# New order tables for TensorE, ScalarE, VectorE and GpSimd in a one-core encoder layer

## The chip, the cores and the metric

The kernel runs on one core of a Trainium2 chip. The metric is the device time of one execution in microseconds; of several executions the median is given. Below, TensorE (PE) does the matrix products, VectorE (DVE), ScalarE (ACT) and GpSimd (POOL) the elementwise work, and SyncE (SP) issues nearly all transfers between the core's memory and DRAM.

## The reference

One layer of an encoder for 1024 new frames ("prompt") and 64 further frames ("sample") that attend to a cache of 512, width 1024, all in float32. Cut to what matters:

```
z = x @ w_in                       # 1024 -> six fox heads (q, k, v, forget gate), u and v of a gated
                                   # unit, six stick-breaking heads (q, k, v)
o_f = softmax(q k / 8 + c_q - c_k) v          # c = cumsum of log forget gates, causal
o_s = sigmoid(z) * prod(1 - sigmoid(later z)) v   # stick-breaking weights, strictly causal
o_g = gelu(u) * (tril(w_s) layer_norm(gelu(v)) + b_s)   # within chunks of 128 positions
o   = rms_norm_per_head([o_f, o_g, o_s]) * g_mix
x   = layer_norm(ALPHA * x + o @ w_out)
h   = square(relu(x @ w_up))                  # 1024 -> 4096
y   = layer_norm(ALPHA * x + h @ w_down)      # 4096 -> 1024
```

Outputs are y for both groups of frames, the new keys and values, the log forget gates and the gated unit's v.

## The kernel before

Every float32 factor is split in a high and a low part, and a product is three passes on TensorE (`PASSES`, L23): high by high, high by low, low by high. ScalarE writes the high part (L1507, L1790), VectorE or GpSimd subtracts it to get the low part (`lo_sub`, L327).

The program is one function, `_build`, whose stages follow one another in time with some overlap:

- 0 to about 520 us: input projection (L613), attention of both kinds (scores L813, transposes L861, products with the values L871 to L874) and the gated unit;
- 520 to 620 us: output projection (L485), residual and first layer norm;
- 620 to 980 us: the up projection (L1569). The 4096 columns go in 16 groups of 256. The frames are in two parts, x = 0 with 288 rows of a product's output and x = 1 with 256. A group's 2 by 2 blocks are multiplied in seven products instead of eight, `PROD` (L1547), into four PSUM accumulators zA to zD per group and part;
- 980 to 1311 us: the down projection (L2034) in a similar scheme, with sums in `acc`;
- to the end: second layer norm of the last tiles and their stores.

The names in the rows below say group and part: zD4_0 is accumulator D of group 4, part 0. In the up stage, `Chain.product` issues the twelve matmuls of a product and then evacuates. The first two products into zA are copied by ScalarE to sn (L1580), the third to a plane of hh for part 0, else to sn (L1580 too). zB is added to sn by VectorE (L1585), zC is subtracted (L1587). zD holds two products in turn: after the first, VectorE adds it to the third copy (L1583), and then the second is accumulated onto it and evacuated by L1589. So the second product into a zD can't start before L1583 has read it. Then relu and square (L1601), four sums and differences of planes (L1610 to L1613), and stores of the planes to DRAM by SyncE (L1614, L1615, L1618), from where the down stage loads them. The buffers hh and sn are used again by later groups, so an evacuation can wait for a store to land. Weights are loaded to wr (L1759), summed by VectorE (L1516 to L1520), and split to wa (ScalarE, GpSimd) and ws (ScalarE L1790, VectorE L327).

In the tail, VectorE adds the last product to acc with a row sum (L2044), takes the negative mean (L2108), ScalarE sums the squares (L2113), GpSimd computes the scale (L2103, L2104) and the shift (L2124), and the row is normalised either by ScalarE (L2128) and GpSimd (L2132, L2136) or by VectorE in two steps (L2144, L2146). Each finished piece is stored (L2137, L2147).

What sets the order: the code emits instructions in a natural order, and at its end `_build` walks five tables, one for each engine, which are a permutation written out by hand of a planner. A word "n+k" takes n instructions in turn that stand at place k of those left. Each instruction is tied to the one before it on its engine:

```python
        for word in ORDER[eng].split():
            n, k = (int(x or d) for x, d in zip(re.match(r"(\d*)\+?(\d*)", word).groups(), (1, 0)))
            for _ in range(n):
                i = left.pop(k)
                if prev is not None:
                    tc.add_manual_dep(i, prev.name, ...)
```

An engine executes its instructions in that order and stops at one whose inputs or buffers aren't ready. The change touches only the tables.

Of the kernel before, what the change touches and what calls it, by code (L numbers as in the profile page):

```python
# [50 lines left out]
12 8+12 28 8+8 9 +27 +23 1 2+22 +23 2+51 2 2+21 3 +46 +44 +17 8 +35 4 +31 +5 4 +26 1 +25 4 +49 3 +2 +41 1 +1 1  # L51
+38 2+14 +38 +36 +65 1 +35 2+13 6 +27 1 2+53 +26 1 +51 2 7+3 1 12+2 +57 2+29 2 +27 +55 +84 1 +54 +26 +50 +52
2+50 +77 +8 8 2+17 1 +16 +37 +16 1 +15 14 5+1 +41 5+1 2+36 18 9+2 5 +4 3 +1 2 3+28 5+24 32 8+2 10 8+1 6+9 2+1
+3 2+8 16+6 +3 +5 +3 7+4 +1 1 +1 33 8+2 7+4 1 2+15 +3 4+14 1 3+13 2+14 1 3+69 11+13 1 2+12 +11 5+54 13+59 2+3
+9 2+7 3+54 3 4+9 2+13 1 +3 1 2+10 2+2 4+14 2 +6 15+31 1 +30 +17 +29 3+5 1 2+25 1 +24 1 2+11 2 +9 2+2 2+11 +2
+10 1 +11 +9 4+1 4+6 1 +4 2+9 2 2+7 5 2+2 2+10 2 +8 4+28 2+8 5 6+23 +21 +22 +21 3 7+2 1 5+1 +26 +10 2+1 +3 +25
+1 1 8+10 +16 2+12 +13 1 +12 +7 6+11 1 3+18 2+9 3+3 2+13 1 +12 +2 +4 1 +9 +3 +8 7+14 +8 1 +10 +11 8+18 +7 +21
+10 2+3 +5 +2 +4 2+15 +2 +3 +36 1 2+1 +33 +10 1 3+31 +9 +30 +1 +8 +1 6+27 +1 2+6 2+8 1 +5 16+6 2+16 +22 1 +21
+5 1 +13 2+163 +13 3+3 +29 2+32 2 +12 +26 4+1 +24 +1 2+21 +7 +13 +1 +18 +1 3+139 1 3+138 5+140 +4 3+139 +19 +4
2 +2 +5 +2 3+132 +4 +12 +14 2 +10 +2 +9 4+124 3+9 +121 3+122 3+2 2+12 4+2 2+8 4+111 3+8 +2 1 3+106 1 +14 +5 3  # L60
+2 3+9 +96 +2 4+95 2+2 +6 +2 +5 +90 3+32 +2 +31 +4 +30 3+4 +27 2+4 5+2 2+3 +2 2+17 +2 10+66 +10 1 2+1 7+62 2+1
1 +4 3+8 2+4 2+6 1 7+50 3 2+2 +45 +2 +44 +2 2+45 3+6 1 4+1 2 2+38 2 2+2 2 +24 3 2+32 +21 +6 1 +5 2 3+26 +3 +25
+3 5+24 +44 +24 +79 +50 +24 +77 +42 +48 +3 +74 2+41 2+23 1 +69 +42 +22 +12 +14 1 +38 +19 1 4+61 6+18 2+12 +16
+52 +33 +51 1 3+15 1 +14 3 +24 2 2+31 +22 2+30 1 +2 2+32 +2 +19 12+30 2+60 +30 1 +12 1 +4 +26 +10 18+25 +35
# [2360 lines left out]
```

## Time and profile before

| | before |
|---|---|
| median of 3 runs | 1329.39 us (1329.36 to 1331.23) |
| profiled execution | 1324.07 us |
| its span, first to last instruction | 1322.3 us |
| TensorE busy | 1289.6 us, 98%, 8851 matmuls |
| VectorE busy | 973.0 us, 74% |
| ScalarE busy | 722.0 us, 55% |
| GpSimd busy | 601.1 us, 45% |
| mean granted TensorE clock | 0.996 |

Times in rows are microseconds from the start of the span. The profiled execution is 5.3 us shorter than the median of the others. Busy time of TensorE counts its matmuls, not its weight loads, which overlap them. A name in brackets behind an idle time is that of the instruction or transfer that ended it.

### The profile page before, as it was taken

How to read it: one execution, taken by the hardware profiler on the slowest of the kernel's cores; microseconds unless marked ns; L12 is line 12 of the kernel's file. 1: busy time of each engine (PE TensorE's matmuls, PEld its weight loads, DVE VectorE, ACT ScalarE, POOL GpSimd, SP SyncE). 2: the span in 40 equal slices, each digit the busy share in tenths (PEclk: the TensorE clock that was granted, in tenths of full speed). 3: DMA queues.
4: the chain of work that ended last, by engine and by line, in shares of the span. 5: the costliest groups of instructions: out<-in, count | busy, mean ns of one | idle time of the engine just before them, and what ended most of it. 6: DMA issues, size and time to landing. Idle time of an engine off the chain costs nothing.

```text
span 1322.3 us, 24296 instructions
## 1 busy us (share of the span) xinstructions
PE 1289.6 (98%) x8851; PEld 1185.5 (90%) x8851; DVE 973.0 (74%) x1800; ACT 722.0 (55%) x1560; POOL 601.1 (45%) x670
## 2 busy tenths in 40 slices
PE   8999999999999999999999999999999999999996
PEld 8999989999988998878999999999978888888885
DVE  4678666677896587898877576757677777676777
ACT  4467576677675575344433222222357676676775
POOL 2231222255785555865322122221177666574657
PEclk9999999999999999999999999999999999999998
DMA  7445574231413357431334434443667443444433
GB/s 232 118 131 155 173 210 123 75 79 47 110 30 88 91 182 274 125 127 60 112 119 143 156 126 147 146 140 131 217 229 264 142 153 113 166 135 148 134 129 136
DMA packets 158048, 185.64 MB, mean 140 GB/s; under 512 B 27740, under 2 KB 116124, under 8 KB 157928
## 3 DMA queue, kind: packets, MB, share of 16 engines
q1 hardware_dynamic: 155832, 183.01, 43.9%
q8 instruction: 70, 1.15, 0.4%
q10 hardware_dynamic: 2096, 1.07, 0.3%
q14 instruction: 50, 0.41, 0.1%
HBM read 117.65 MB, written 60.10 MB: 134 GB/s over the span
## 4 chain that ended last, share of the span: by engine, by line
PE 78%; DVE 8%; DMA 6%; ACT 3%; POOL 3%; issue 2%; SPq 1%; DVEq 0%; ACTq 0%; POOLq 0%
PE A L2034 12%; PE zA L1569 8%; PE mx L485 7%; PE zD L1569 6%; PE kvsb L613 5%; PE D L2034 5%; PE zC L1569 3%; PE zB L1569 3%; PE B L2034 3%; PE kvfox L613 2%; PE qsb L753 2%; PE Ssb L813 2%; PE sgu L613 2%; PE Sfox L813 2%; PE qfox L753 2%
## 5 line engine op out<-in xcount | busy, mean ns | idle before, releaser
L327 POOL TENSOR_TENSOR wa<-wr,wa 128x512 fp32r<-128x512 f32 x41 | 60.9, 1509 | 236.6 <-ACT wa L1507 236.5
L327 POOL TENSOR_TENSOR wd<-rd,wd 128x512 fp32r<-128x512 f32 x77 | 105.8, 1383 | 111.1 <-ACT wd L1507 90.9
L1569 PE MATMUL zD<-xo,ws 128*128 128x256 f32 (+1 forms) x720 | 126.7, 288 | 4.9 <-DVE hh L1583 4.9
L1569 PE MATMUL zA<-xo,ws 128*128 128x288 f32 (+1 forms) x720 | 120.0, 288 | 0.9 <-ACT sn L1580 0.5
L1569 PEld LDWEIGHTS zD<-xo,ws 128*128 128x128 f32 x720 | 104.6, 188 | 6.7 <-DVE hh L1583 6.4
L485 PE MATMUL mx<-xT,oTb 128*128 128x512 f32 (+1 forms) x416 | 105.4, 402 | 0.0
L1569 PEld LDWEIGHTS zA<-xo,ws 128*128 128x128 f32 x720 | 102.1, 188 | 2.0 <-ACT sn L1580 1.6
L613 PE MATMUL kvfox<-wkvfox,xT 128*128 128x256 f32 (+3 forms) x624 | 98.1, 293 | 1.8 <-ACT wkvfox L586 0.8
L613 PE MATMUL kvsb<-wkvsb,xT 128*128 128x256 f32 (+1 forms) x624 | 99.2, 290 | 0.4 <-ACT wkvsb L586 0.3
L1580 ACT ACTIVATE sn<-zA 128x256 f32<-128x256 f32 (+1 forms) x80 | 31.0, 392 | 110.3 <-PE zA L1569 91.4
L2034 PE MATMUL A<-wd,wd 128*128 128x512 f32 x312 | 89.5, 390 | 0.1
L485 PEld LDWEIGHTS mx<-xT,oTb 128*128 128x128 f32 (+1 forms) x416 | 74.3, 186 | 16.1
L613 PEld LDWEIGHTS kvfox<-wkvfox,xT 128*128 128x128 f32 (+1 forms) x624 | 83.3, 187 | 3.0 <-ACT kvsfox L714 1.1
L613 PEld LDWEIGHTS kvsb<-wkvsb,xT 128*128 128x128 f32 (+1 forms) x624 | 83.8, 187 | 0.8 <-ACT wkvsb L586 0.5
L1507 ACT ACTIVATE wd<-rd 128x512 fp32r<-128x512 f32 x105 | 63.8, 622 | 32.2 <-DMA rd<-w_down 19.1
L799 POOL TENSOR_TENSOR sgsb<-sgsb,snsb 128x127 f32<-128x127 f32 (+7 forms) x48 | 60.2, 1256 | 45.0 <-DVE snsb L797 33.6
L1701 POOL TENSOR_TENSOR rd<-rd 128x512 f32<-128x512 f32 x56 | 74.6, 1331 | 6.9 <-DVE b L327 4.7
L2034 PE MATMUL A<-wd,h4a 128*128 128x512 f32 x240 | 74.5, 391 | 0.8 <-ACT p L2051 0.5
L1569 PE MATMUL zB<-xo,wa 128*128 128x288 f32 (+1 forms) x360 | 74.3, 287 | 0.0
L797 DVE TENSOR_TENSOR_SCAN snsb<-snsb,one 128x128 f32<-128x128 f32 (+7 forms) x48 | 67.4, 1412 | 6.8 <-ACT snsb L796 6.3
L1569 PE MATMUL zC<-xo,wa 128*128 128x288 f32 (+1 forms) x360 | 72.4, 287 | 0.0
L2034 PEld LDWEIGHTS A<-wd,wd 128*128 128x128 f32 x312 | 58.5, 188 | 13.5 <-DVE acc L1999 0.5
(560 smaller groups left out, 3896.2 us busy)
## 6 DMA issues: line engine op xcount, KB each, us to landing
h_dr<-hh SPq DMA_DIRECT2D x30, 512.0 KB, 3.2
rd<-w_down SPq DMA_DIRECT2D x30, 512.0 KB, 4.6
wr<-w_up SPq DMA_DIRECT2D x13, 1024.0 KB, 5.7
hr<-h_dr SPq DMA_DIRECT2D x31, 384.0 KB, 3.5
h_dr<-hh SPq DMA_DIRECT2D x30, 384.0 KB, 3.6
raw<-w_in SPq DMA_DIRECT2D x44, 256.0 KB, 3.4
wo_dr<-swo SPq DMA_DIRECT2D x32, 256.0 KB, 2.5
xT<-wo_dr SPq DMA_DIRECT2D x8, 1024.0 KB, 7.5
```

Source lines behind the costliest of these rows:

```text
L327: eng.tensor_tensor(out, src, hi.bitcast(F32), op=ALU.subtract)
L485: nc.tensor.matmul(acc[0:m], oT[:, k, hx, 0:m], wo[k // 4][hw][:, k % 4, cs], start=(i == 0), stop=(i == len(seq) - 1))
L613: nc.tensor.matmul(acc[0:n, c0:c0 + n1 - n0], xT[k // 4][:, k % 4, c:c + n], wt[:, k, hw, n0:n1], start=(i == 0), stop=(i == len(seq) - 1))
L753: nc.tensor.matmul(acc[:, 0:w], wq[:, k, hw, :], xT[k // 4][:, k % 4, c:c + w], start=(i == 0), stop=(i == len(seq) - 1))
L797: nc.vector.tensor_tensor_scan(g[:, 0:n][:, ::-1], g[:, 0:n][:, ::-1], one.broadcast_to([P, n]), 1.0, op0=ALU.mult, op1=ALU.bypass)
L799: nc.gpsimd.tensor_tensor(s[:, 0:n - 1], s[:, 0:n - 1], g[:, 1:n], op=ALU.mult)
L813: nc.tensor.matmul(sps[:, b0 - c0:b0 - c0 + n], qd[:, h, s, half * P:(half + 1) * P], kp[b0 // 256][:, h, 0:n], start=(s == 0), stop=(s == ...
L1507: nc.scalar.activation(hi, raw, AF.Copy)
L1569: nc.tensor.matmul(z, w[:, hw, k], xop(s, bo, hx)[:, k, :], start=(new and k == 0 and j == 0), stop=(k == 3 and j == 2), skip_group_check= ...
L1580: nc.scalar.activation(c, z, AF.Copy)
L1701: eng.tensor_tensor(r[:, o], r[:, x], r[:, y], op=ALU.subtract)
L2034: nc.tensor.matmul(z, h[:, hx, q, o], wset[self.c % 2][q][:, hw, wb], start=((n in (0, 3) or n == 1 and self.c == 0) and q == 0 and j == 0 ...
```

## The change

The tables of TensorE, ScalarE, VectorE and GpSimd are replaced; SyncE's table and all other code stay. The number of words changes from 3825 to 4338 (TensorE), 1174 to 1167 (ScalarE), 1343 to 1323 (VectorE) and 403 to 410 (GpSimd). All instructions are the same ones; the code below the tables moves 15 lines down, so that L1583 is L1598 in the new kernel. The diff, of which a row tells nothing by itself:

```diff
 ORDER = {}
 ORDER["PE"] = """
-12 8+12 28 8+8 9 +27 +23 1 2+22 +23 2+51 2 2+21 3 +46 +44 +17 8 +35 4 +31 +5 4 +26 1 +25 4 +49 3 +2 +41 1 +1 1
...
+15 3+9 +10 4+9 23 6+10 1 +39 2+35 +9 +36 +34 +10 +34 +33 +10 3+9 1 13+8 10 +32 1 +34 1 +3 +59 2+29 3 +26 8 +2
...
 """
 ORDER["ACT"] = """
...
 ORDER["DVE"] = """
...
 ORDER["POOL"] = """
...
 ORDER["SP"] = """
```

The new tables were planned with the latest landings of four executions and up to the last store instead of TensorE's last product. What they move is shown at three places. A row is line, operation, output <- inputs, shape, and a count where it stands several times in a row; the number behind a name is only the tile's.

VectorE at the change from group 3 to group 4 of the up stage, 724 to 733 us before (ws5 is the split weight sum of group 5), before:

```order
L1612 TENSOR_TENSOR hh3_0_9664<-hh3_0_9664 128x256
L1612 TENSOR_TENSOR hh3_1_9666<-hh3_1_9666 128x256
L327 TENSOR_TENSOR ws5_9885<-wr5_9872,ws5_9885 128x2048
L1585 TENSOR_TENSOR hh4_1_9892<-zB4_1_9935,sn4_1_9891 128x256
L1583 TENSOR_TENSOR hh4_0_9890<-zD4_0_9975,hh4_0_9890 128x288
L1583 TENSOR_TENSOR hh4_1_9892<-zD4_1_9988,sn4_1_9891 128x256
L1587 TENSOR_TENSOR hh4_0_9890<-hh4_0_9890,zC4_0_10029 128x288
L1585 TENSOR_TENSOR hh4_0_9890<-zB4_0_9921,sn4_0_9889 128x288
```

and now:

```order
L1627 TENSOR_TENSOR hh3_1_9666<-hh3_1_9666 128x256
L342 TENSOR_TENSOR ws5_9885<-wr5_9872,ws5_9885 128x2048
L1598 TENSOR_TENSOR hh4_0_9890<-zD4_0_9975,hh4_0_9890 128x288
L1598 TENSOR_TENSOR hh4_1_9892<-zD4_1_9988,sn4_1_9891 128x256
L1600 TENSOR_TENSOR hh4_1_9892<-zB4_1_9935,sn4_1_9891 128x256
L1600 TENSOR_TENSOR hh4_0_9890<-zB4_0_9921,sn4_0_9889 128x288
L1602 TENSOR_TENSOR hh4_0_9890<-hh4_0_9890,zC4_0_10029 128x288
```

The evacuation of zD4_0 (128x288) stands ahead of all work of part 1 now, and behind it first the evacuation of zD4_1, then the two of zB.

VectorE at the change from group 7 to group 8, 809 to 818 us before (the two planes and ws9 stand ahead of the evacuation of zD8_0), before:

```order
L1612 TENSOR_TENSOR hh7_1_10570<-hh7_1_10570 128x256
L1520 TENSOR_TENSOR wr9_10776<-wr9_10776 128x4x128
L1613 TENSOR_TENSOR hh7_0_10568<-hh7_0_10568 128x256
L1611 TENSOR_TENSOR hh7_0_10568<-hh7_0_10568 128x256
L1612 TENSOR_TENSOR hh7_0_10568<-hh7_0_10568 128x256
L327 TENSOR_TENSOR ws9_10789<-wr9_10776,ws9_10789 128x2048
L1583 TENSOR_TENSOR hh8_0_10794<-zD8_0_10879,hh8_0_10794 128x288
```

and now:

```order
L1535 TENSOR_TENSOR wr9_10776<-wr9_10776 128x4x128
L1628 TENSOR_TENSOR hh7_0_10568<-hh7_0_10568 128x256
L1627 TENSOR_TENSOR hh7_0_10568<-hh7_0_10568 128x256
L1628 TENSOR_TENSOR hh7_1_10570<-hh7_1_10570 128x256
L1627 TENSOR_TENSOR hh7_1_10570<-hh7_1_10570 128x256
L342 TENSOR_TENSOR ws9_10789<-wr9_10776,ws9_10789 128x2048
L1598 TENSOR_TENSOR hh8_0_10794<-zD8_0_10879,hh8_0_10794 128x288
```

The four last subtractions are those of both parts in turn; the two last were part 0's and are part 1's now.

ScalarE around the third product of zA15_1, 952 to 959 us before (h4a, st and wd are operands of the down stage, sn15_1 the copies of zA15_1), before:

```order
L1580 ACTIVATE hh14_0_12246<-zA14_0_12247 128x288
L1580 ACTIVATE sn15_1_12353<-zA15_1_12355 128x256 x2
L1728 ACTIVATE h4a_12369<-h4a_12369 128x512 x2
L1732 ACTIVATE st1_12443<-h4a_12369 128x512
L1728 ACTIVATE h4a_12369<-h4a_12369 128x512
L1580 ACTIVATE sn15_1_12353<-zA15_1_12355 128x256
L1507 ACTIVATE wd0_0_12493<-rd0_0_12296 128x512 x2
```

and now:

```order
L1595 ACTIVATE hh14_0_12246<-zA14_0_12247 128x288
L1595 ACTIVATE sn15_1_12353<-zA15_1_12355 128x256 x2
L1743 ACTIVATE h4a_12369<-h4a_12369 128x512
L1595 ACTIVATE sn15_1_12353<-zA15_1_12355 128x256
L1747 ACTIVATE st1_12443<-h4a_12369 128x512
L1522 ACTIVATE wd0_0_12493<-rd0_0_12296 128x512 x2
L1743 ACTIVATE h4a_12369<-h4a_12369 128x512 x2
```

The third copy stood behind three preparations of the down stage and stands behind one now.

In the tail two things move. On VectorE, among the last ten rows, a 512-wide first step (L2144) of the last tile, which stood third from the end, now stands ahead of the two second steps (L2146) of the tile before it, and a 256-wide first step moves from ahead of these to behind them. On GpSimd, the addition to another tile (L2136), which stood behind a scale that waits for ScalarE near 1302 us, stands ahead of it now.

425 rows, old and new, of the table ORDER are left out of this document.

## The prediction

> **What bounds the kernel now.** I read the stage table first: busy time of each engine, stretch by stretch. Columns: stretch, its length, busy us (and instructions) of TensorE, its weight loads, VectorE, ScalarE and GpSimd, then the granted clock, the DMA share and GB/s.
>
> ```profile
> 0.00:40.00 40.00, 36.35 (x286) 34.91 (x287) 19.55 (x42) 18.21 (x39) 9.85 (x34) 1.00 0.68 202
> 40.00:350.00 310.00, 306.37 (x2551) 299.59 (x2550) 222.89 (x546) 201.52 (x500) 108.94 (x186) 1.00 0.44 125
> 350.00:520.00 170.00, 163.04 (x1310) 155.91 (x1309) 128.16 (x230) 108.36 (x274) 103.64 (x126) 0.99 0.42 128
> 520.00:620.00 100.00, 100.00 (x499) 80.28 (x498) 85.10 (x150) 39.77 (x69) 68.37 (x72) 1.00 0.35 110
> 620.00:980.00 360.00, 353.45 (x2769) 347.63 (x2769) 259.89 (x411) 120.43 (x226) 90.70 (x65) 1.00 0.44 143
> 980.00:1310.70 330.70, 330.43 (x1447) 267.16 (x1445) 249.64 (x412) 230.99 (x452) 213.38 (x179) 1.00 0.47 157
> 1310.70:1322.30 11.60, 0.00 (x0) 0.00 (x0) 7.78 (x14) 2.77 (x5) 6.18 (x11) 0.71 0.61 226
> ```
>
> TensorE is the bound, at nearly full clock. No matmul is added or removed, so an order can change only its idle time: per stage (length less busy) 3.65, 3.63, 6.96, 0.00, 6.55 and 0.27 us, and the 11.60 us behind its last product. That makes 32.66 of the span's 1322.3 us, 2.5%, and nothing that this change does can earn more. The next view is TensorE's waits by releaser (us in total, times, longest):
>
> ```profile
> PE zD L1569 <- DVE hh L1583: 4.9, 5, 1.9
> ```
>
> Three quarters of the idle time of the MLP's up stage (4.9 of 6.55 us) has one cause: an accumulator zD whose earlier product VectorE hasn't yet evacuated. Three of the five waits, at 732.71, 817.69 and 959.20 us, make 4.41 us. I followed each back on the engines' timelines (start, length, engine, line, operation, tiles, shape, count, and in brackets the idle time ahead with its releaser).
>
> **The change part by part.** It permutes instructions on four engines; SyncE's queue keeps its order, so no store or load moves past another on it. A row that was split costs nothing, as TensorE's own rows show where products alternate:
>
> ```profile
> 727.34 0.28 PE L1569 MATMUL zC<-xo,wa 128*128 128x256 f32 x1
> 727.46 0.30 PE L1569 MATMUL zB<-xo,wa 128*128 128x288 f32 x1
> 727.59 2.26 PE L1569 MATMUL zA<-xo,ws 128*128 128x256 f32 x17
> 729.69 0.62 PE L1569 MATMUL zD<-xo,ws 128*128 128x256 f32 x4
> ```
>
> ```profile
> 730.71 0.55 PE L1569 MATMUL zC<-xo,wa 128*128 128x288 f32 x3
> 732.71 0.51 PE L1569 MATMUL zD<-xo,ws 128*128 128x288 f32 x2 [1.44 <-DVE hh L1583]
> ```
>
> Starts lie 0.12 and 0.13 us apart where each product goes to another accumulator, and (729.69 − 727.59) / 17 = 0.12 us inside a run on one. Term for more switches: 0.
>
> *Place 1, 732.71 us.* TensorE idles 1.44 us for the evacuation of zD4_0. What stood ahead of it:
>
> ```profile
> 725.97 2.29 DVE L327 TENSOR_TENSOR ws<-wr,ws 128x2048 fp32r<-128x2048 f32 x1 [0.78 <-ACT ws L1790]
> 731.86 0.42 DVE L1585 TENSOR_TENSOR hh<-zB,sn 128x256 f32<-128x256 f32 x1 [3.60 <-DMA h_dr<-hh]
> 732.20 0.45 DVE L1583 TENSOR_TENSOR hh<-zD,hh 128x288 f32<-128x288 f32 x1
> ```
>
> ```profile
> 728.96 0.41 ACT L1580 ACTIVATE hh<-zA 128x288 f32<-128x288 f32 x1 [3.03 <-PE zA L1569]
> ```
>
> ```profile
> 726.33 5.41 DMA h_dr<-hh
> ```
>
> The L1583 at 732.20 needs zD4_0 and ScalarE's copy, ready at 728.96 + 0.41 = 729.4. It ran 2.8 us later because the L1585 ahead of it, of the other token pair, writes a buffer whose store took 5.41 us to land, at 731.74: blocking at the head of a queue. In the new order hh4_0<-zD4_0 stands directly behind the 2.29 us subtraction, which ends at 728.3, and the instruction that waits for the landing (now hh4_1<-zD4_1) behind it. The evacuation then ends near 729.4 + 0.5 = 729.9, TensorE wanted it at 732.71 − 1.44 = 731.27, and it has about the same products ahead. Gain 1.4 us, bounds 0 and 1.44. Next late is hh4_1<-zD4_1, which still waits for 731.74; by the order TensorE needs its bank some twenty 0.13 us products, 2.6 us, after the first, so it is covered, narrowly.
>
> *Place 2, 817.69 us*, the longest wait:
>
> ```profile
> 815.47 0.29 PE L1569 MATMUL zB<-xo,wa 128*128 128x288 f32 x1
> 817.69 1.19 PE L1569 MATMUL zD<-xo,ws 128*128 128x288 f32 x7 [1.92 <-DVE hh L1583]
> ```
>
> ```profile
> 816.74 0.41 ACT L1580 ACTIVATE hh<-zA 128x288 f32<-128x288 f32 x1 [4.12 <-DMA h_dr<-hh]
> ```
>
> ```profile
> 817.18 0.46 DVE L1583 TENSOR_TENSOR hh<-zD,hh 128x288 f32<-128x288 f32 x1 [2.24 <-ACT hh L1580]
> ```
>
> ```profile
> 812.87 3.76 DMA h_dr<-hh
> ```
>
> Here the store of hh7_0 itself is late: issued at 812.87, landed at 816.63, and ScalarE, VectorE and TensorE follow one after another. Its last plane subtraction was VectorE's last before the 2.29 us weight split; now two subtractions of 0.42 us, those of hh7_1, follow it, so it can be issued about 0.8 us earlier. TensorE's order also gives it about six more products (0.8 us) ahead of the bank that waits. Together 1.6 of 1.92 us if both hold; the order of the stores on SyncE is unchanged, so a store of hh7_1 can stand ahead and eat some of it. I take 1.2, bounds 0.8 and 1.92.
>
> *Place 3, 959.20 us:*
>
> ```profile
> 959.20 1.64 PE L1569 MATMUL zD<-xo,ws 128*128 128x256 f32 x12 [1.05 <-DVE hh L1583]
> ```
>
> ```profile
> 956.87 0.62 ACT L1728 ACTIVATE h4a<-h4a 128x512 fp32r<-128x512 f32 x1
> 957.39 0.37 ACT L1580 ACTIVATE sn<-zA 128x256 f32<-128x256 f32 x1
> ```
>
> ```profile
> 958.72 0.42 DVE L1583 TENSOR_TENSOR hh<-zD,sn 128x256 f32<-128x256 f32 x1
> ```
>
> ScalarE's evacuation sn15_1<-zA15_1 stood behind three preparations of the down stage (L1728, L1732, L1728, 0.6 us each); now only one L1728 is between it and its fellows. That is 1.2 us on ScalarE, and zA15_1's products end about 1.1 us earlier. Gain 1.0 of 1.05.
>
> *Small waits.* The stage table for four shorter stretches:
>
> ```profile
> 505.00:510.00 5.00, 3.35 (x26) 2.78 (x25) 4.68 (x10) 2.13 (x6) 3.60 (x4) 1.00 0.76 239
> 510.00:513.60 3.60, 3.54 (x16) 3.21 (x16) 3.03 (x6) 1.63 (x6) 3.26 (x5) 0.53 0.99 369
> 655.00:665.00 10.00, 9.06 (x67) 8.39 (x67) 5.06 (x12) 2.25 (x5) 0.69 (x1) 1.00 0.89 270
> 969.00:987.00 18.00, 16.90 (x81) 12.93 (x80) 14.52 (x20) 7.17 (x15) 12.68 (x8) 1.00 0.57 196
> ```
>
> From 969 to 987 TensorE idles 1.10 us; the products that wait for ScalarE stand about 3 us later now, gain 0.7 (bounds 0, 1.1). From 655 to 665 it idles 0.94; VectorE's second weight split stands 15 rows earlier, gain 0.5 (0, 0.94). The end of the attention is different: from 505 to 510 VectorE is busy 4.68 of 5 us, and its rows stand in nearly the old order, so most of the 6.96 us of that stage stays. After the 1.65 idle us the clock is granted at 0.53 for 3.6 us, which costs 3.6 × 0.47 = 1.7 us more. One evacuation stands three rows earlier; gain 0.7, bounds 0 and 2.5 (half of the five's idle time and the clock's 1.7). In the first 350 us a transposition is moved 2 us later and little else: 0.5 of 7.28 idle us, bounds 0 and 1.0.
>
> [...]
>
> *Tail.*
>
> ```profile
> 1314.54 0.74 DVE L2146 SCALAR_TENSOR_TENSOR acc<-acc,ident,gbp 128x512 f32<-128x512 f32 x1
> 1315.88 1.41 DVE L2146 SCALAR_TENSOR_TENSOR acc<-acc,ident,gbp 128x512 f32<-128x512 f32 x2 [0.59 <-POOL ident L2104]
> ```
>
> ```profile
> 1302.18 0.19 POOL L2103 TENSOR_SCALAR ident<-ident 128x1 f32<-128x1 f32 x1 [0.69 <-ACT hx L2113]
> ```
>
> ```profile
> 1315.29 0.55 POOL L2104 TENSOR_TENSOR ident<-ident,negh 128x1 f32<-128x1 f32 x1
> ```
>
> Behind the last product VectorE does the same operations as before. It waits 0.59 us for GpSimd's last scale. Now a 512-wide L2144 (0.74) stands before that point in place of a 256-wide one, which takes about 0.3 of the wait; and GpSimd, whose work from 1302.18 on runs without a pause, begins a 1024-wide addition before the 0.69 us wait rather than behind it, so the scale comes about 0.5 us earlier. Gain 0.5, bounds 0 and 0.59. The other 11 us are products' remains, VectorE's operations and a store, and stay.
>
> *New waits.* The 360 us of the up stage are ordered anew on TensorE in nearly every group, and no row shows which buffer will be late. Bounds from other stages' idle shares: 0.27 / 330.7 = 0.08% (0.3 us) and 3.63 / 310 = 1.2% (4.2 us); a negative cost is excluded, since every wait that can vanish is counted above. In between I take 2.0, as the old order of the same stage has 1.75 us beside the 4.8 counted out (6.55 − 1.4 − 1.2 − 1.0 − 0.7 − 0.5).
>
> **Sum.** −1.4 − 1.2 − 1.0 − 0.7 − 0.5 − 0.7 − 0.5 − 0.5 + 2.0 = −4.5 us. The profiled execution took 1324.07 us (span 1322.3 and 1.8 around it), so 1319.6 would stand in its place. The median of the runs shown, 1329.39, lies 5.32 above it; I carry that over: **1324.9 us**, with 1322 to 1326.7 as this case's own range.
>
> **The rivals.**
>
> *A larger gain (0.10).* The 5.32 us between profile and median must be waits that this trace doesn't have, transfers that land later than here. At place 1 a later landing holds up whatever is blocked behind it one for one; where the waiting instruction now stands last, that cost goes too. If half of the 5.3 goes, 1324.9 − 2.7 = 1322. Against it: SyncE's order and the bytes are unchanged, and the attention, with the largest idle time, hardly changes.
>
> *Nothing moves in sum (0.28).* Gains at three places are real, but each next evacuation is narrow: at place 1 the 731.74 landing still holds hh4_1, zB4_1 and zB4_0, all behind it now. If the new waits are 4.2 and the small waits give nothing, −1.4 − 1.2 − 1.0 − 0.5 + 4.2 = +0.1 us: 1329.5.
>
> *Slower through VectorE and GpSimd at once (0.20).* Both read the same memory, and rows show a price:
>
> ```profile
> L1601 DVE SCALAR_TENSOR_TENSOR hh<-hh x30: 1210/1358/2362, 668.5 to 986.1; 128x1152 f32<-128x1152 f32 x15, 128x1024 f32<-128x1024 f32 x15
> ```
>
> ```profile
> 801.60 4.61 DVE L1601 SCALAR_TENSOR_TENSOR hh<-hh 128x1152 f32<-128x1152 f32 x2
> ```
>
> ```profile
> 801.45 5.91 POOL L327 TENSOR_TENSOR wa<-wr,wa 128x512 fp32r<-128x512 f32 x3 [18.69 <-ACT wa L1507]
> ```
>
> Two squares that take 1.36 us as a median take 2.3 each beside GpSimd's three subtractions, 1.0 more apiece. The new order starts squares earlier, straight behind the first token pair's evacuations, where ScalarE's splits, which release GpSimd, also fall. Each collision delays the planes, their stores and the next evacuation. Seven more on a waited-for path use up 4.5 + 2.66 us; with nine the sum is +4.5: 1333.9. Against it: VectorE is busy 259.89 of the stage's 360 us, so most squares have slack, and the median shows that most run at full speed now.
>
> [...]
>
> That the change doesn't do what it says would show as the old order on an engine; the rows that moved exclude that.
>
> **How the numbers follow.** A measurement tells 0.2%, 2.66 us, from no change: faster is below 1326.7, slower above 1332.1. The forecast has 0.42, the larger gain 0.10, nothing moved 0.28, slower 0.20. So faster 0.52, same 0.28, slower 0.20. The range is 1318.0 to 1333.5: below, all gains at their bounds with 0.3 of new waits (−1.44 − 1.92 − 1.05 − 1.1 − 0.94 − 2.5 − 1.0 − 0.59 + 0.3 = −10.2, 1319.1) and a little of the larger gain; above, most of the slower case.
>
> **What would show it.** In the changed profile: the waits of zD for the evacuation (L1583, fifteen lines further down there) fall from 4.9 us to under 2; VectorE near 730 us has the 128x288 evacuation before the wait for h_dr; TensorE is busy about 357 of 360 us from 620 on (353.45 + 4.8 − 2.0 = 356.3 of the same work); no 0.59 us wait in the tail; the clock still dips once before 515. It is wrong if new waits for sn or hh exceed 4 us, if a dozen squares take 2.3 us, or if the attention's order, though alike, meets other landings.

## The result: 14 to 16 us faster, three times the forecast

| | before | changed | ratio (95% interval) |
|---|---|---|---|
| median of four runs | 1329.38 us | 1313.58 us | 0.9881 (0.9863 to 0.9900) |
| second comparison, another chip | 1325.33 us | 1311.39 us | 0.9887 (0.9874 to 0.9901) |
| third comparison, another chip | 1325.66 us | 1311.41 us | 0.9893 (0.9876 to 0.9909) |
| first profiled execution | 1324.07 us, span 1322.3 | 1314.50 us, span 1312.8 | |
| second profiled execution | 1323.92 us, span 1322.2 | 1311.93 us, span 1310.2 | |

The forecast of 1324.9 us was wrong, and so was its range, 1318.0 to 1333.5. The sign was right; the size is beyond even the case called "a larger gain" (1322 us), which had a chance of 0.10.

The stage table of the changed kernel's first profile (columns as in the prediction; all line numbers of the changed kernel are 15 higher):

```profile
0.00:40.00 40.00, 37.89 (x296) 36.98 (x297) 20.16 (x42) 18.13 (x39) 10.17 (x34) 1.00 0.70 210
40.00:350.00 310.00, 305.57 (x2570) 301.24 (x2568) 226.02 (x549) 204.84 (x506) 109.85 (x186) 1.00 0.44 125
350.00:520.00 170.00, 161.41 (x1278) 154.79 (x1277) 123.89 (x227) 106.45 (x266) 103.37 (x126) 0.97 0.42 128
520.00:620.00 100.00, 100.00 (x500) 79.90 (x499) 85.14 (x147) 39.79 (x68) 72.34 (x73) 1.00 0.34 110
620.00:980.00 360.00, 358.83 (x2805) 354.22 (x2804) 268.21 (x423) 124.60 (x232) 94.70 (x69) 1.00 0.45 150
980.00:1301.00 321.00, 321.00 (x1413) 261.26 (x1411) 239.47 (x400) 229.98 (x447) 203.05 (x175) 1.00 0.45 152
1301.00:1312.80 11.80, 0.26 (x2) 0.00 (x0) 7.83 (x15) 3.08 (x5) 6.28 (x11) 0.60 0.66 244
```

Two things are to be seen. TensorE's idle time from 620 to 980 us went from 6.55 to 1.17 us; the idle time of the stages ahead of it and of the tail did not improve. And the idle time in sum fell by only 32.7 − (1312.8 − 1285.0) = 4.9 us, though the span fell by 9.5. The other half is busy time: 1289.6 us before, 1285.0 now, for the same 8851 products.

A clean account needs no busy time. The two orders cut the program at some points into the same sets of products, so the times at which that many products have started can be compared directly. They are read from TensorE's own starts in each trace, in us from the start of the span; a row gives the start of the product that follows that many (the last row, that of the last one):

| products started | before | before, 2nd | changed | changed, 2nd | changed, 3rd |
|---|---|---|---|---|---|
| 4660 (up stage begins) | 625.1 | 624.5 | 625.2 | 622.3 | 623.5 |
| 5501 | 733.2 | 732.3 | 730.8 | 727.8 | 729.0 |
| 6183 | 820.4 | 819.6 | 816.7 | 813.8 | 814.8 |
| 7155 | 942.1 | 940.6 | 937.2 | 934.3 | 935.3 |
| 7510 (down stage alone) | 1004.8 | 1004.1 | 996.0 | 993.2 | 994.2 |
| 8851 (the last) | 1310.3 | 1310.3 | 1300.9 | 1298.3 | 1300.1 |
| end of span | 1322.3 | 1322.2 | 1312.8 | 1310.2 | 1312.0 |

From the 4660th to the 7510th product the old order takes 379.8 and 379.6 us, the new one 370.8, 370.9 and 370.7: 8.7 to 9.1 us less in every pair of profiles, 8.9 in the mean. That is five sixths of the mean 10.6 us between the spans. Ahead of it 1.1 us are won in the mean (within what one profile differs from another), behind it 0.5, and in the tail 0.1.

What became of the waits of the up stage: TensorE's waits from 620 to 1310 us, in the second profile of the changed kernel (us in total, times, longest).

```profile
PE zD L1584 <- DVE hh L1598: 0.6, 1, 0.6
PE zA L1584 <- ACT sn L1595: 0.4, 1, 0.4
PE xtc L1458 <- DVE h L1602: 0.2, 1, 0.2
```

Five waits for zD with 4.9 us have become one with 0.6. Place 1 looks as forecast, VectorE in the changed kernel's first profile:

```profile
724.61 2.28 DVE L342 TENSOR_TENSOR ws<-wr,ws 128x2048 fp32r<-128x2048 f32 x1
729.92 0.46 DVE L1598 TENSOR_TENSOR hh<-zD,hh 128x288 f32<-128x288 f32 x1 [3.03 <-PE zD L1584]
731.41 0.42 DVE L1598 TENSOR_TENSOR hh<-zD,sn 128x256 f32<-128x256 f32 x1 [1.03 <-ACT sn L1595]
731.75 0.78 DVE L1600 TENSOR_TENSOR hh<-zB,sn 128x256 f32<-128x256 f32 x2
```

Behind the weight split VectorE now waits 3.03 us for TensorE's product instead of 3.60 for a store's landing. It is early, and TensorE doesn't wait for it.

### The price of a wait

The missing half is in rows that the prediction quoted. Before the wait of place 1, three products start at 730.71, at 0.13 us each. The fourth could have started at 731.11 and started at 732.71: 1.60 us late, where the row says 1.44 us idle. A product lasts 0.28 us as recorded but gives way to the next after 0.12 or 0.13, so the first 0.16 us of the wait lie under the last product and count as busy. The restart costs once more, as the row behind the wait shows in the kernel before:

```profile
732.71 0.51 PE L1569 MATMUL zD<-xo,ws 128*128 128x288 f32 x2 [1.44 <-DVE hh L1583]
733.06 0.73 PE L1569 MATMUL zC<-xo,wa 128*128 128x256 f32 x5
```

Two products, the second one 256 wide (it goes to another zD), take 733.06 − 732.71 = 0.35 us instead of 0.25. So this wait costs 1.44 + 0.16 + 0.10 = 1.70 us. The waits of the stage read the same way by their starts, on other shapes too: 0.30 us idle at 970.36 is 0.46 late and 0.11 at the restart, 0.24 us idle at 971.33 is 0.41 late and 0.11 at the restart. These waits cost their idle time and about 0.27 us each. From the same figures it is estimated that a wait shorter than 0.16 us costs up to 0.27 us and shows as no idle time.

The count closes the account. From the 4660th to the 7510th product the first trace before has 15 products with some idle time ahead of them, 6.67 us in sum, and the changed kernel's first has four with 1.17. Eleven fewer at 0.27 us make 3.0 of the 9.0 − 5.5 = 3.5 us that the idle time doesn't hold between these two. (In the second trace before they are 14 with 7.32 us: ten fewer make 2.7 of 8.9 − 6.2 = 2.7 us.) The little that is left fits waits too short to show: products that start more than 0.06 us later than usual with no idle time ahead of them (those right behind a wait left out) are 23 before, 2.1 us late in sum, and 15 now, 1.4 us. One stands at 984.81 us before, 0.10 us late.

Why a product gives way to the next 0.16 us before its recorded end, and why the one behind a wait gives way 0.1 us late, no run here shows.

### The profile page after: what moved, and what is told of

It is laid out like the page before. It is cut to its first block, busy times and chain, and to the rows that moved or that the text cites. A ratio compares the mean times of both kernels' runs of the same rounds, so it can differ in the third digit from the quotient of the medians.

```text
span 1312.8 us, 24315 instructions
## 1 busy us (share of the span) xinstructions
PE 1285.0 (98%) x8851; PEld 1188.4 (91%) x8851; DVE 970.7 (74%) x1800; ACT 726.9 (55%) x1560; POOL 599.8 (46%) x670
## 4 chain that ended last, share of the span: by engine, by line
PE 82%; DVE 6%; DMA 4%; POOL 3%; ACT 2%; issue 2%; SPq 0%; DVEq 0%; ACTq 0%; POOLq 0%
PE A L2049 12%; PE zA L1584 10%; PE mx L500 7%; PE zD L1584 7%; PE D L2049 6%; PE kvsb L628 5%; PE kvfox L628 4%; PE zB L1584 3%; PE zC L1584 3%; PE B L2049 3%; PE qsb L768 2%; PE Sfox L828 2%; PE qfox L768 2%; PE sgu L628 2%; PE ptfox L876 1%
## 5 line engine op out<-in xcount | busy, mean ns | idle before, releaser
L342 POOL TENSOR_TENSOR wd<-rd,wd 128x512 fp32r<-128x512 f32 x77 | 102.3, 1334 | 113.7 <-ACT wd L1522 103.3
L1584 PE MATMUL zD<-xo,ws 128*128 128x256 f32 (+1 forms) x720 | 135.6, 287 | 0.6 <-DVE hh L1598 0.6
L1584 PE MATMUL zA<-xo,ws 128*128 128x288 f32 (+1 forms) x720 | 127.1, 288 | 0.4 <-ACT sn L1595 0.3
L1584 PEld LDWEIGHTS zD<-xo,ws 128*128 128x128 f32 x720 | 108.8, 188 | 0.9 <-DVE hh L1598 0.8
L500 PE MATMUL mx<-xT,oTb 128*128 128x512 f32 (+1 forms) x416 | 108.8, 408 | 0.0
L1584 PEld LDWEIGHTS zA<-xo,ws 128*128 128x128 f32 x720 | 105.4, 188 | 0.9 <-ACT sn L1595 0.9
L1584 PE MATMUL zB<-xo,wa 128*128 128x288 f32 (+1 forms) x360 | 79.5, 287 | 0.0
L1716 POOL TENSOR_TENSOR rd<-rd 128x512 f32<-128x512 f32 x56 | 74.0, 1322 | 10.3 <-DVE b L342 6.5
L1584 PE MATMUL zC<-xo,wa 128*128 128x288 f32 (+1 forms) x360 | 77.5, 287 | 0.0
L2016 DVE TENSOR_TENSOR acc<-acc,A 128x512 f32<-128x512 f32 x73 | 49.6, 683 | 33.9 <-PE A L2049 33.6
L812 DVE TENSOR_TENSOR_SCAN snsb<-snsb,one 128x256 f32<-128x256 f32 (+7 forms) x48 | 67.9, 1423 | 7.5 <-ACT snsb L811 6.7
```

The source lines that it names most:

```text
L342: eng.tensor_tensor(out, src, hi.bitcast(F32), op=ALU.subtract)
L500: nc.tensor.matmul(acc[0:m], oT[:, k, hx, 0:m], wo[k // 4][hw][:, k % 4, cs], start=(i == 0), stop=(i == len(seq) - 1))
L812: nc.vector.tensor_tensor_scan(g[:, 0:n][:, ::-1], g[:, 0:n][:, ::-1], one.broadcast_to([P, n]), 1.0, op0=ALU.mult, op1=ALU.bypass)
L1584: nc.tensor.matmul(z, w[:, hw, k], xop(s, bo, hx)[:, k, :], start=(new and k == 0 and j == 0), stop=(k == 3 and j == 2), skip_group_check= ...
L1716: eng.tensor_tensor(r[:, o], r[:, x], r[:, y], op=ALU.subtract)
L2016: nc.vector.tensor_tensor(out, out if other is None else other, bank, op=ALU.add)
```

## The experiments

All kernels with another order use the same machinery: tables spliced from the old and the new ones at points where both have executed the same instructions on each engine. The two main cuts lie at about 625 and 1008 us:

```python
c0 = dict(PE=4660, ACT=832,  DVE=888,  POOL=405)   # about 625 us
cm = dict(PE=6183, ACT=949,  DVE=1112, POOL=438)   # about 820 us
c1 = dict(PE=7516, ACT=1091, DVE=1328, POOL=486)   # about 1008 us
```

### Which stage

The first comparison ran the kernel before for a second profile and three splices.

```diff
# up_new
+order[e] = old[e][:c0[e]] + new[e][c0[e]:c1[e]] + old[e][c1[e]:]
# up_old
+order[e] = new[e][:c0[e]] + old[e][c0[e]:c1[e]] + new[e][c1[e]:]
# att_old
+order[e] = old[e][:c0[e]] + new[e][c0[e]:]
```

The kernel before, unchanged:

> The kernel before, unchanged, for a second profile. In the first, whose execution took 1324.07 us, TensorE idled 6.55 us from 620 to 980 us; the median of four others is 1329.38. Theory A (the old order loses most of the gain of 15.8 us in the up stage, and in most executions more than the first profile showed): a profile of an execution near 1329 us has about 10 to 12 us of idle time in 620 to 980 and other stages within 1 us of the first. Theory B (the 5.3 us between the first profile and the median lie elsewhere, in the attention or its clock): 620 to 980 idles 6 to 7 us again and 350 to 520 about 12.

1324.64 us against 1326.35 of the kernel before beside it, ratio 0.9994 (0.9981 to 1.0006). The two are one and the same kernel, so two medians differ by 1.7 us here without any change; smaller differences below are read with the ratio's interval and the traces. Its profile, of an execution of 1323.92 us, repeats the first one's waits for zD (4.9 us) to 0.3 us:

```profile
PE zD L1569 <- DVE hh L1583: 5.2, 5, 2.0
```

The up stage loses nearly the same in both profiles (6.55 and 6.65 us of idle time from 620 to 980), so these waits follow the order and were not chance of one execution. That is theory B's figure for the up stage, but 350 to 520 us idled 7.2 us and not 12. Theory A could not be tried, since the profiled execution was again a short one.

> The new order from 625 to about 1008 us (the up stage) on all four engines, the old order before and after it. Theory A: 12 to 14 of the 15.8 us come from here: 1315 to 1317.5 us. Theory B (each stage brings what the two profiles show, 7.9 us here): about 1321.5 us. A third, that the new order of the stages ahead sets when the up stage's loads land: under 3 us of gain, 1326.5 or more.

1318.52 us, ratio 0.9944 (0.9926 to 0.9962), 7.8 us less than before: between theories A and B, and the third fell.

> The complement: the old order from 625 to about 1008 us, the new one before and after. Theory A: 1326.5 to 1328 us. Theory B: 1321 to 1322 us. The third theory: 1316 us or less.

1322.70 us, ratio 0.9979 (0.9966 to 0.9991), 3.7 us less by the medians and 2.8 by the ratio: nearest to theory B. Its profiled execution was the longest of its ten, with a span of 1323.6 us, no shorter than before: the old up stage took 382.9 us there, 3 more than in the kernel before, of which a stretch of 3.4 us at half the clock, at 817 us, explains 1.7 at most.

> The old order up to 625 us (projection, attention, mixer), the new one from there to the end. Theory A: 1313 to 1315 us, near the full change, as nothing much is won ahead of 625; the attention's 350 to 520 us idled 8.59 us in the new profile against 6.96 in the old and had the clock at 0.97 instead of 0.99, so 1 to 3 us less than the full change, 1311 to 1313, is possible. Theory B: 1317 to 1319, if the 5.3 us between profile and median lie ahead of 625 and are lost again.

1314.44 us, ratio 0.9919 (0.9897 to 0.9940), 11.9 us less, as theory A has it.

The up stage holds most of the gain. The order ahead of it matters little: the kernel with the old one there has a span of 1312.9 us, the three of the full change 1310.2 to 1312.8, though its ratio leaves 3 to 5 us, with intervals that overlap. But the parts don't add up: with the new up stage, making the down stage new too brings another 4.1 us by the medians (1318.52 to 1314.44; the ratios' intervals overlap). In the profile of the kernel with the new up stage alone the 7510th product starts at 996.6, as in the full change, yet 308.9 us pass to the last one, instead of 305.4 and 306.2 in the kernel before and 304.9 to 305.9 in the changed one. Its waits from 980 us:

```profile
PE A L2034 <- DVE acc L2001: 0.8, 1, 0.8
PE ds L2078 <- POOL hs L327: 0.4, 1, 0.4
PE A L2034 <- ACT wd L1507: 0.3, 1, 0.3
PE A L2034 <- ACT p L2051: 0.2, 1, 0.2
```

The old down stage, arriving 8 us early, waits on a chain that starts with a load of weights (issued at 1124.30, landed 7.24 us later), goes over ScalarE and VectorE, and holds TensorE until 1136.54. The new order is not free of it: the third profile of the changed kernel has one such wait too, 0.7 us on the same chain, and that of the kernel with the old order up to 625 us has one of 1.1 us on another. From the 7510th product to the last, in all profiles but those with late landings:

| order of the down stage | us |
|---|---|
| old, reached at 1004 and 1005 us | 305.4, 306.2 |
| old, reached 1 to 8 us earlier (four kernels) | 307.1, 307.2, 307.9, 308.9 |
| new (eight profiles) | 304.9 to 305.2 six times, 305.9, 306.5 |

So the down stage has next to no time of its own to win, but by the old order it gives back 1 to 3 us of what an earlier stage wins.

### Piece by piece

The second comparison ran the full change again and three smaller pieces.

```diff
# place1: old tables, and on VectorE at 732 us
-hh4_1<-zB4_1 (L1585)
 hh4_0<-zD4_0 (L1583)
+hh4_1<-zB4_1 (L1585)
# half1
+order[e] = old[e][:c0[e]] + new[e][c0[e]:cm[e]] + old[e][cm[e]:]
# down_new
+order[e] = old[e][:c1[e]] + new[e][c1[e]:]
```

> The full change again, beside the kernels of the last comparison (there the kernel before took 1326.35 us and the one with only the attention old 1314.44). If the gain is what the two profiles show (9.6 us, of which 9.2 lie between 625 and 1005 us) plus the 1 to 2 us by which ordinary executions of the kernel before exceed its profiled one: 1314 to 1316. If the new order tolerates late landings that cost the old one 15.8 us in the first comparison wherever it runs: 1310 to 1312.

1311.39 us, 13.9 less than before. That is more than the 12.0 us between the two second profiles. The median of the kernel before lies 0.7 to 5.3 us above its profiled executions in all comparisons, that of the changed one 0.5 to 2.4 below its own. Against the 10.6 us between the spans, the medians differ by 5.2, 3.4 and 3.7 us more in the three comparisons. Single executions spread about as widely (1322.6 to 1331.2 us before, 1308.7 to 1314.5 now), so part of it is luck in which execution was profiled; what an ordinary execution does differently is in no trace.

> The kernel before with one pair of instructions exchanged on VectorE: the evacuation of zD4_0 ahead of that of zB4_1, which waits for a store (place 1 of the prediction). Theory of the prediction: the wait of 1.44 us at 732.71 goes (1.6 us from start to start of the products), 1.4 to 1.6 us less. Rival: the next evacuation (zD4_1, still behind the landing) waits instead, gain under 0.5 us. The profile shows which: the start of the product behind it near 731.1 or near 732.7.

1324.72 us, ratio 0.9990 (0.9981 to 0.9999), 0.6 us less by the medians and 1.3 by the ratio. TensorE and VectorE in its profile:

```profile
730.17 0.75 PE L1569 MATMUL zC<-xo,wa 128*128 128x256 f32 x5
730.76 0.29 PE L1569 MATMUL zA<-xo,wa 128*128 128x288 f32 x1
730.89 0.80 PE L1569 MATMUL zD<-xo,ws 128*128 128x288 f32 x5
```

```profile
728.22 0.46 DVE L1583 TENSOR_TENSOR hh<-zD,hh 128x288 f32<-128x288 f32 x1 [1.15 <-ACT hh L1580]
730.24 0.42 DVE L1585 TENSOR_TENSOR hh<-zB,sn 128x256 f32<-128x256 f32 x1 [1.57 <-DMA h_dr<-hh]
```

The wait is gone without a trace, and the landing that VectorE still waits for holds up no product: the product that had started at 732.71 starts at 730.89, without idle time. The blocking at the head of the queue was read rightly. From 4660 to 5501 products the kernel takes 106.5 us instead of 108.1 and 107.8. But the span is no shorter than before: 733 to 820 takes 0.8 us more, and the old down stage, reached 1 to 2 us earlier, waits more:

```profile
1141.41 1.66 PE L2034 MATMUL A<-wd,wd 128*128 128x512 f32 x6 [0.69 <-DVE acc L2001]
```

This is the same chain again as above (here the load was issued at 1129.86 and took 6.57 us). So of the 1.3 to 1.6 us that the first stretch wins the span shows nothing, and the 0.6 or 1.3 us of the medians is not clear of what two medians of one kernel differ by. A wait removed alone is worth what the stages behind it let through.

> The new order from 625 to 820 us only. In the profiles TensorE loses 6.4 us there by the old order against nominal spacing (4.5 up to 733, 1.9 up to 820) and 2.4 to 3.1 by the new one. Theory 1 (gains pass through): 3.5 to 4 us less than before. Theory 2 (the old order behind it is planned for the old times and gives part back, as it seemed to do in the down stage behind the new up stage): 1 to 2 us less.

1320.09 us, ratio 0.9953 (0.9940 to 0.9967), 5.2 us less: above both theories. In its profile 625 to 820 takes 192.1 us instead of 195.3 and 195.1, 3.1 us less, the down stage gives 1 to 1.6 back, and the span (1319.1) is 3.1 us shorter, just under theory 1; the other 2 us are the difference between median and profile again.

> The old order up to 1008 us and the new one from there (down projection and tail). Theory 1 (the down stage of the old order loses time only when it starts earlier than planned): 0 to 0.7 us less than before, as the two profiles differ by 0.6 us there. Theory 2 (the new order of the down stage is itself worth the 4.1 us between the kernel with the new up stage alone and the one with all new from 625 us on): 3 to 4 us less.

1323.50 us, ratio 0.9981 (0.9971 to 0.9990), 1.8 us less. Between the theories and nearer the first; its profile ends at 1322.4, where the kernel before ended at 1322.3 and 1322.2, so where ordinary executions win this is not seen, and it is no more than two medians of the kernel before differed by.

### Undoing, the last third, and filling waits

```diff
# undo1: new tables, and on VectorE
+hh4_1<-zB4_1
 hh4_0<-zD4_0
 hh4_1<-zD4_1
-hh4_1<-zB4_1
# half2
+order[e] = old[e][:cm[e]] + new[e][cm[e]:c1[e]] + old[e][c1[e]:]
# att_fill: new tables, and on TensorE at 16 waits ahead of 560 us
+(1 to 8 later products of another accumulator)
 the waiting product
```

> The full change once more, only so that the three kernels below have it beside them: 13 to 15 us less than before.

1311.41 us, 14.2 less than before.

> The full change with place 1 undone on VectorE: the evacuation of zB4_1, which waits for the landing of a store, again ahead of that of zD4_0. Theory (each wait costs the idle time that the profile shows and 0.27 us more, and place 1 is worth what its exchange in the old order brought): 1.3 to 1.7 us more than the full change, and a wait of zD reappears near 728 us. Rival (the gain is TensorE's new order, which has enough other products ahead of the second product into zD4_0): under 0.4 us, no such wait.

1310.47 us, ratio 0.9886 (0.9871 to 0.9900): no loss. The theory fell. VectorE there:

```profile
719.09 2.28 DVE L327 TENSOR_TENSOR ws<-wr,ws 128x2048 fp32r<-128x2048 f32 x1
723.95 0.42 DVE L1585 TENSOR_TENSOR hh<-zB,sn 128x256 f32<-128x256 f32 x1 [2.57 <-PE zA L1569]
724.68 0.46 DVE L1583 TENSOR_TENSOR hh<-zD,hh 128x288 f32<-128x288 f32 x1 [0.30 <-PE zD L1569]
```

and SyncE's stores of the group ahead:

```profile
718.20 0.51 SPq L1615 DMA_DIRECT2D h_dr<-hh  x1
718.80 0.58 SPq L1614 DMA_DIRECT2D h_dr<-hh  x1
719.47 0.53 SPq L1615 DMA_DIRECT2D h_dr<-hh  x1
```

With the old exchange back, the evacuation of zB4_1 is released by TensorE and no longer by the landing. Two things differ from the old order. The landing: the last store was issued at 719.47, so it landed within 4.5 us, where the old order's took 5.41; there four stores left within 2.4 us, and here the first had left at 712.62, 6.9 us before the last. And TensorE's order: the last matmul of zD4_0's first product starts at 724.29, 2.9 us behind the end of VectorE's weight split, where the old order starts it at 726.33, 1.9 us ahead of that end. The old order's first and last store, in the kernel before:

```profile
723.98 0.52 SPq L1614 DMA_DIRECT2D h_dr<-hh  x1
...
726.33 0.97 SPq L1615 DMA_DIRECT2D h_dr<-hh  x1
```

So the result is the one that the rival (TensorE's new order) forecast, and the stores may have their part in it; the two were not separated. The second product into zD4_0 starts at 725.30, 0.16 us behind the end of the evacuation, so there is not much room. The exchange is sufficient in the old order and not necessary in the new.

> The new order from 820 to 1008 us only. By start-to-start excess in the profiles the old order loses 5.6 us there (4.7 of it from 942 to 1005, where its idle time is only 2.2) and the new one 0.2. Theory (the excess counts): 4 to 5.4 us less than before, less up to 2 that the old down stage gives back. Rival (the idle time counts): 2 to 2.5 us less.

1320.66 us, ratio 0.9958 (0.9941 to 0.9974), 5.0 us less (3.4 to 7.8 by the interval): the theory that counts starts, not idle time. By its profile 942 to 1005 takes 58.0 us instead of 62.7 and 63.5, 4.7 and 5.5 us less, where the old order's idle time was 2.2 and 3.3 us. (Its span, 1318.8, is 3.4 us shorter; the old down stage takes 307.2 us behind it.) This stretch has only waits of 0.1 to 0.3 us beside place 3, so the hidden price weighs most there.

> The full change with TensorE's order alone altered ahead of 560 us: at 16 waits that both profiles of the full change show (from 45 to 500 us, 8.4 us of idle time), 1 to 8 later products of another accumulator are moved ahead of the waiting one, 6.8 us of products in all. Theory (a filled wait brings its idle time and up to 0.27 us): 4 to 8 us less than the full change. Rival (in the attention VectorE, busy up to 94%, sets the pace and the wait only moves on to the next product): within 1.5 us of the full change.

1310.07 us, ratio 0.9883 (0.9868 to 0.9898), 1.3 less than the full change beside it, with intervals that overlap: the theory's 4 us did not come, and the median agrees with the rival. Its 4660th product starts at 620.9 us in the profile, against 622.3 to 625.2 in the three of the full change; but the kernel with place 1 undone, whose order up to there is the full change's own, shows 620.1. The clock blurs this: TensorE ran at half the clock for 6.8 us from 503.2 here, which costs 3.4 us at most; the kernel with place 1 undone has no such stretch. At the 4070th product, ahead of that stretch and behind all the fills, the times are 499.5 with the fills and 500.8 to 503.6 without them in four profiles. So the fills may have won 1 to 4 us; this isn't settled. One of the fills, ahead of 171 us, shows how a wait moves on:

```profile
171.22 0.33 PE L873 MATMUL ofox<-pthfox,vpfox 128*128 128x128 f32 x1 [1.53 <-DVE pthfox L327]
```

The product pulled forward reads what VectorE writes (pthfox), and that wasn't ready: the wait is now its own, 1.53 us, where the full change waited 0.37, 0.34 and 0.40 at three products nearby (second profile). That VectorE paces the attention agrees with it and isn't shown by one place, where the fill itself wasn't ready.

### Late landings

What was open was whether the new order wins by tolerance: it was planned with the latest landings of four executions. Two kernels make the landings late.

```diff
             nc.sync.dma_start(h4_dr[p, s], self.hh(0, 4)[:, :, 0:2 * P])
+            nc.sync.dma_start(spare_dr[p, s], self.hh(0, 4)[:, :, 0:2 * P])
```

> The kernel before, with each store of the first four planes of hh (512 KB) issued twice, the second time to a spare buffer, directly ahead of the store of the other planes (31 stores more): so every later landing of the up stage comes some 1 to 3 us later. Theory (the old order has evacuations queued right behind a landing, so it loses nearly one for one at each of the places, and the new order was planned for later landings): 6 to 15 us more than before. Rival (landings have slack in both orders): under 3 us more.

> The full change with the same second stores. Theory: at most 4 us more than the full change, so that the two orders lie 18 to 25 us apart instead of 14. Rival (the new order has no more tolerance than the old; it only removes the waits of the landings as they are): it loses as much as the old order does, and the distance stays 12 to 16 us.

The old order took 1351.37 us, ratio 1.0187 (1.0165 to 1.0209), 25.9 more than before. The new one took 1340.42, 15.0 more than before and 29.0 more than the full change of the third comparison. The distance shrank from 14 to 11 us where the theory had 18 to 25, so the theory fell; it is also just under the rival's 12 to 16. By the traces both up stages lose alike: from the 4660th to the 7510th product the old order takes 408.8 us and the new one 398.4, 29.0 and 27.6 more than without the second stores. The profiles' transfer tables show how late the stores became (KB each, median us from issue to landing), first the old order, then the new:

```profile
spare_dr<-hh SPq DMA_DIRECT2D x30, 512.0 KB, 4.2
h_dr<-hh SPq DMA_DIRECT2D x30, 384.0 KB, 4.6
```

```profile
h_dr<-hh SPq DMA_DIRECT2D x30, 384.0 KB, 4.9
```

Without the second stores the 384 KB took 3.6 and 3.8 us. Landings about one us slower, and issued behind one more store (the like 512 KB store beside it took 0.52 us of issue in the median), cost 26 and 29 us by the medians over 32 stores (one for each of 16 groups and two parts, not 31), 0.8 and 0.9 us for each. Not all of it is waiting: the granted clock is 0.98 in this stage of both, with stretches at half the clock of 17.1 us in sum in the old order (8.5 us at most) and 13.7 in the new (6.8), where no trace without the second stores has more than 3.4 us. TensorE's waits, old order, then new:

```profile
PE zD L1568 <- DVE hh L1582: 15.7, 11, 4.9
PE zB L1568 <- DVE hh L1584: 3.5, 2, 2.9
```

```profile
PE zA L1568 <- ACT hh L1579: 8.7, 4, 4.2
PE zD L1568 <- DVE hh L1582: 4.7, 3, 2.2
```

The new order fits the landings as they are; with landings this late it loses as the old one does, at other accumulators. Smaller delays, of some tenths of a us, were not tried, so a tolerance of that size stays possible.

## Why the prediction was wrong, step by step

The forecast's sum was −4.5 us against the profiled execution, carried over to the median. The spans of two profiles before and three after give −10.6 in the mean, the medians −15.8, −13.9 and −14.2.

| step, as the prediction put it | forecast | measured |
|---|---|---|
| places 1, 2, 3 (idle 4.41) | −1.4, −1.2, −1.0 | all three waits gone, −4.4 idle |
| small waits 655 to 665 and 969 to 987 (idle 2.04) | −0.5, −0.7 | gone, −2.0 idle |
| new waits in the up stage | +2.0 | +1.2 idle, four waits (0.20, 0.28, 0.13, 0.57); 0.2 of other old ones gone |
| price of a wait beyond its idle time | not seen | −3.5 (−2.7 from the second profile before) |
| attention and the first 350 us | −0.7, −0.5 | −1.1 in the mean, within what profiles differ |
| down stage | 0 | −0.5; old order reached early: +1 to +3 |
| tail | −0.5 | −0.1 (VectorE's last operation −0.5) |
| median like the profile | carried over, +5.32 | before 0.7 to 5.3 above its profiles, changed below its own |

**The first step that failed is the cost of each wait**, taken as the idle time of TensorE's rows: "an order can change only its idle time". Busy time fell by 4.6 us with the same products. The price left out about 3 us of the up stage's 8.9. Next to it stand the two hedges: 4.8 us of the 6.5 counted waits where all went, and 2.0 of new ones where 1.2 came. Together the up stage was forecast at −2.8 and brought −8.9; with that the forecast would have been 1318.8 us.

**The second is the carry-over**: the median was taken to lie 5.32 us above the profile for the changed kernel as for the old one. The changed kernel's median lay 0.5 to 2.4 us below its profiles. So the medians fell by 5.2 us more than the profiles in the first comparison, and by 3.4 and 3.7 in the others. This took the result out of the range, which 1318.8 is still in. Its cause stays open.

**Place 1 was right as a mechanism**, and shown by exchanging two instructions in the old order. That this exchange is what the change wins there was wrong: undone in the new order it costs nothing, as TensorE's products into zD4_0 come later against VectorE's rows there and the store lands sooner; which of the two it is was not separated. Places 2 and 3 were not tried alone; their waits are gone.

**No term spoke of the stage behind.** The prediction took the down stage's 0.27 idle us as nothing to win. It has next to none to win, but 1 to 3 us to lose when it is reached earlier: its own waits appear then, as the profiles of four kernels show. New tables for it kept most of the gain.

**The clock** was forecast to dip once before 515 us. The changed kernel's first profile has stretches at half the clock at 385 us (3.4 us, granted 0.50 from 385.1 to 388.4) and 508 us (6.8 us, granted 0.50 from 508.0 to 514.8), the second has none, the third one at 506 us (6.8 us). The rows from 500 to 520 us, first and second profile:

```profile
500.00:520.00 20.00, 17.28 (x95) 14.72 (x95) 15.31 (x30) 9.52 (x23) 14.49 (x15) 0.83 0.88 301
```

```profile
500.00:520.00 20.00, 17.47 (x106) 14.59 (x107) 16.15 (x30) 9.41 (x22) 16.28 (x16) 1.00 0.83 287
```

The same order has the dip in one execution and not in the other, at nearly the same busy time; the first is 2.9 us later at the 4660th product, and its two stretches cost 5.1 us at most. From 505 to 510 us, by the prediction's row, TensorE was busy 3.35 of 5 us, 67%; over the 3.4 us just ahead of the dip there (as long as the dip, granted 0.50 from 510.1 to 513.5) it was busy 51% and 52% in the two profiles before, and 52%, 54% and 56% ahead of those of the changed kernel. Whether a low busy share brings the dip, and from which share on, that doesn't show, nor why one execution has the dip and another of the same order hasn't. That it would go with the idle time ahead of it, as the bound of 2.5 us has it, was the author's estimate.

**The tail** went as forecast on VectorE and not at the end. VectorE in the changed kernel's first profile:

```profile
1306.35 1.41 DVE L2161 SCALAR_TENSOR_TENSOR acc<-acc,ident,gbp 128x512 f32<-128x512 f32 x2 [0.28 <-POOL ident L2119]
1307.67 0.47 DVE L2159 SCALAR_TENSOR_TENSOR acc<-acc,ident,gbp 128x256 f32<-128x256 f32 x1
1308.06 1.13 DVE L2161 SCALAR_TENSOR_TENSOR acc<-acc,ident,gbp 128x512 f32<-128x512 f32 x2
```

Its last operation ends at 1309.19, 7.9 us behind the last product's end at 1301.26, where it was 8.4 (1319.11 and 1310.67 before): the 0.5 us of the forecast; the wait for GpSimd's scale is 0.28 instead of 0.59. But the span ends 11.5 us behind that product, after 11.6 before. What ends it is the landing of a store. SyncE's last stores, first before, then now (L2137 and L2152 store GpSimd's last piece, the others VectorE's):

```profile
1317.73 0.40 SPq L2137 DMA_DIRECT2D y_prompt<-acc  x1
1318.75 0.81 SPq L2147 DMA_DIRECT2D y_prompt<-acc  x2
```

```profile
1308.20 0.40 SPq L2152 DMA_DIRECT2D y_prompt<-acc  x1
1308.83 0.84 SPq L2162 DMA_DIRECT2D y_prompt<-acc  x2
```

By the landings in the traces VectorE's last store lands last in all five profiles, and GpSimd's piece 1.0 to 1.2 us ahead of it. That last store was issued 8.5 and 8.4 us behind the last product before and 8.0 now, but landed 10.5 and 10.4 us behind it before and 10.4 now: it takes 2.4 us to land instead of 2.0. So what VectorE gained was lost in the landing; why the landing grew isn't shown.

**The rivals.** *Slower through VectorE and GpSimd at once* did not come. The squares in the changed kernel take 1352 ns in the median, where the prediction's row has 1358:

```profile
L1616 DVE SCALAR_TENSOR_TENSOR hh<-hh x30: 1212/1352/2250, 668.0 to 977.6; 128x1152 f32<-128x1152 f32 x15, 128x1024 f32<-128x1024 f32 x15
```

*The larger gain* was right that the distance between profile and median can go (it took half of the 5.3 us, and 5.2 went in the first comparison), and its ground wasn't borne out. It put the distance on late landings that the new order tolerates; with landings made about one us late, the new order lost as much as the old. What remains open is the 3 to 5 us of the carry-over; splitting them would need traces of long executions of the kernel before.

## What to carry to other kernels

Where products overlap as here (0.28 us long, 0.12 us apart), read a wait from start to start, not from the idle time in brackets: here each cost 0.27 us more, and the many short waits, not the three long ones, held most of what was overlooked. A stage that shows next to no idle time can still lose some when it is reached earlier, as the down stage did by the old order (0.27 us idle as it was, 1 to 3 us given back); so price a change of order through to the end, and plan the stages behind it anew. Don't carry the distance between a profile and a median from one kernel over to another: profile several executions. That removing one cause brings a gain doesn't make it the cause in another order: undo it there too.

## What the runs showed of the hardware that I had not expected

By the 0.28 us length and 0.12 us spacing of a 256-wide product the first 0.16 us of a wait show as no idle time, and the product behind a wait gave way 0.10 or 0.11 us later than usual. One more 512 KB store per group and part, 32 in all and 4.2 us to land in the median, cost 26 us in one order and 29 in the other, slower clock included, though the transfer engines were busy only 44% of the time in that stage before. The same instructions in the same order met stretches at half the clock at two places, at one and at none ahead of the last product in three executions.
